# Latent attention opened in a new order: weight splits, value projections and rope of the first heads

## Chip, cores and metric

One of the cores of a Trainium2 chip runs the whole program. Times are microseconds (us) on the device. TensorE is called PE, VectorE DVE, ScalarE ACT, GpSimd POOL and SyncE SP, as in the profile.

## What is computed

A decoder of three blocks in fp32 for 512 rows of width 1024. The change is in the first mixer, multi-head latent attention with 16 heads, with a 512-wide latent for queries and a 256-wide one for keys and values:

```python
h = x @ w_in                                  # 1024 -> 512 + 256 + 32
c_q, c_kv, k_rope = h[..., :512], h[..., 512:768], h[..., 768:]
q = (rms_norm(c_q, q_norm) @ w_uq).reshape(b, s, 16, 64 + 32)
q = jnp.concatenate([q[..., :64], apply_rope(q[..., 64:], pos)], axis=-1)
kv = (rms_norm(c_kv, kv_norm) @ w_ukv).reshape(b, s, 16, 64 + 64)
k_nope, v = kv[..., :64], kv[..., 64:]
k = jnp.concatenate([k_nope, broadcast(apply_rope(k_rope, pos))], axis=-1)
out = dense_causal_attention(q, k, v, 96 ** -0.5) @ w_o
```

Behind it come a layer norm, cross attention over 256 memory rows and a gated FFN; then a block with sparse top-k attention, and a last one with forgetting attention, pooling and a convolutional FFN.

## The kernel before, in words

Every fp32 product is made of three matmuls (`mm3`, lines 153 to 155) on a high and a low half of each operand. `split` makes the two halves of an activation: a cast on ACT (line 160) and a subtraction on DVE (line 161).

Weights are a list of units (`plan`), each of up to 128x1024. `use()` hands out the next unit; before that it sees that `ahead` more units are prepared and that `dma_ahead` more are under way on SP's queue. Preparing one is a cast on ACT to `wh` (line 121) and a subtraction to `wl` (line 122) on `lo_eng`, which is DVE, and POOL during the attention. The units are in order: eight of w_in, two of the rope part of w_uq (`uu`), the values of heads 0 to 7 (`v`), the keys (`k`), the first block of the queries' plain part (`q`, heads 0 to 3), the values of heads 8 to 15 (in the kernel before they replace `v` when `vproj(1, ...)` first asks for them), and the second query block (heads 4 to 7), which `proj(2)` takes.

`mla` (line 482) loads x as four tiles of 128 rows, `setup` loads the constants, `front` transposes tiles (tp, by matmul with the identity) and multiplies them by w_in into pa and pb, and `norm` makes the RMS-normed rows cn: the squares on ACT, a row of short steps for the reciprocal root on DVE, then cn itself (lines 542 to 545). `back` transposes cn and splits it into cq and ckv. `norm(3)` and `back(3)` are those of the last tile. Then rq (the rope part of all queries, two groups of 256 rows), v (values of heads 0 to 7, four blocks of rows, 24 matmuls) and the rope of the keys and of the first queries (`rope`, line 380: a shuffle, two products, a sum and a split).

`proj(p)` makes the keys and queries of head pair p (qk: 6 + 12 matmuls). In `attention` head h goes through scores s (12 matmuls, line 689), a softmax (reductions on DVE, line 692, exponentials on ACT, line 694, the reciprocal on DVE, line 700, products with it on POOL, line 703, in the tiles P and p), transposes t (line 711) two heads later, and the output o three heads later. Behind the scores of head h, `ahead(h)` calls `proj(h//2+1)` for even h; `fill(h)` then runs the values of heads 8 to 15 as `FILL_V` says.

A scheduler orders the instructions of each engine at build time; on the chip each engine runs its own list in that order.

Of the kernel before, what the change touches and what calls it, by code (L numbers as in the profile page):

```python
# [34 lines left out]
FILL_B = {2: 1, 3: 1, 4: 1, 6: 1, 9: 1, 11: 1, 12: 1, 14: 1, 17: 1, 19: 1, 20: 1, 22: 1, 24: 1, 27: 1, 28: 1}  # L35
FILL_V = {1: (0,), 3: (1,), 4: (2, 3)}
FILL_P = {7: (0,), 8: (1,), 9: (2,), 10: (3,)}
# [27 lines left out]
class K:  # L65
# [314 lines left out]
    def rope(self, src, out, eng):  # L380

        nc = self.nc
        t = self.pg(F, "rp")
        t1, t2 = t[:, 0:512], t[:, 512:1024]
        nc.vector.stream_shuffle(t2, src, [(i + 16) % 32 for i in range(32)])
        eng.tensor_tensor(t1, src, self.cos, op=OP.mult)
        eng.tensor_tensor(t2, t2, self.sin, op=OP.mult)
        nc.vector.tensor_tensor(t1, t1, t2, op=OP.add)
        self.split(out[:, 0], out[:, 1], t1)

# [91 lines left out]
    def mla(self):  # L482
# [3 lines left out]
        for t in range(NT):  # L486
            x = self.pg(F, "x0")
            if t == 0:
                nc.scalar.dma_start(x[:, 512:1024], xd[:, t, 512:1024])
                nc.sync.dma_start(x[:, 0:512], xd[:, t, 0:512])  # L490
            else:
                last = nc.sync.dma_start(x, xd[:, t, :])
            xs.append(x)
            self.load(1 if t == 0 else 8)
            if t == 1:
                self.setup(last)
        us = []
# [19 lines left out]
        def front(ts, then=None):  # L517
            xT = [x0T.pop(t) if t in x0T else tr(t) for t in ts]
            pp = [(self.ps("pa"), self.ps("pb")) for _ in ts]
            for k in range(8):  # L520
                if len(us) == k:
                    us.append(self.use(3))
                u = us[k]
                for x, (pa, pb) in zip(xT, pp):
                    l = [x[0][:, k], x[1][:, k]]
                    self.mm3(pa, l, [u[0][:, 0:512], u[1][:, 0:512]], k == 0, k == 7)
                    self.mm3(pb[:, 0:288], l, [u[0][:, 512:800], u[1][:, 512:800]], k == 0, k == 7)
                if k == 4 and then is not None:
                    x0T[then] = tr(then)
            return pp  # L530
# [38 lines left out]
        self.trig()  # L569
        pp += front((3,))  # L570
        back(2, scr[2])
        prev = norm(3, *pp[3])
        self.ahead, self.dma_ahead = 2, 2
        QF = [[self.pair("qf") for _ in range(2)] for _ in range(2)]
# [4 lines left out]
        ropeq, rps = [], []  # L579
        uu = [self.use(), self.use()]  # L580
        for m in range(4):
            rps.append(self.ps("rq"))
        for g in range(2):
            if g == 1:
                back(3, prev)
            for m in range(4):
                for k in range(4):
                    cc = (m % 2) * 128
                    self.mm3(rps[m][:, g * 256:(g + 1) * 256],
                             [uu[m // 2][0][:, k, cc:cc + 128], uu[m // 2][1][:, k, cc:cc + 128]],  # L590
                             [x[:, g * 256:(g + 1) * 256] for x in cqs[k]], k == 0, k == 3)
            if g == 0:
                st = {n: self.use() for n in ("v", "k", "q")}
        V = {}

        def vproj(h, js=range(NT)):
            if h == 1 and js[0] == 0:
                st["v"] = self.use()
            u = st["v"]
            for j in js:  # L600
                p = self.ps("v")
                c = slice(j * 128, j * 128 + 128)
                for k in range(2):
                    self.mm3(p, [x[:, c] for x in ckvs[k]], [u[0][:, k], u[1][:, k]], k == 0, k == 1)
                V[h, j] = self.pair("v")
                self.split(V[h, j][:, 0], V[h, j][:, 1], p)

        kr = self.pair("kr")
        self.rope(krf, kr, nc.vector)
        rsb = [self.pg(F, "rsb") for _ in range(2)]  # L610
        rsb = [rsb[m // 2][:, (m % 2) * 512:(m % 2) * 512 + 512] for m in range(4)]

        def ropes(m):
            rq = self.pair("rq")
            self.rope(rsb[m], rq, nc.vector if m == 0 else nc.gpsimd)
            ropeq.append(rq)
        nc.scalar.copy(rsb[0], rps[0])
        ropes(0)
        for m in range(1, 4):
            nc.scalar.copy(rsb[m], rps[m])  # L620
        for i in range(2):
            nc.scalar.dma_start(KF[i][0][64:96].bitcast(F), kr[64:96].bitcast(F))
            nc.scalar.dma_start(KF[i][1][32:64].bitcast(F), kr[32:64].bitcast(F))
        OT = []
        vproj(0)

# [26 lines left out]
        def ahead(h):  # L653
            if h in (0, 4, 8):
                ropes(h // 4 + 1)
            if h % 2 == 0 and h < 14:
                proj(h // 2 + 1)
        proj(0)
        self.lo_eng = nc.gpsimd

# [1042 lines left out]
```

## Time and profile before

| | us |
|---|---|
| median of 3 runs | 2175.67 |
| lowest and highest | 2175.51, 2180.46 |
| profiled execution | 2170.42 |
| its span | 2168.6 |
| PE busy in it | 2125.2 (98%) |
| DVE, ACT, POOL busy | 1324.1, 925.7, 287.9 |

The profiled execution is one run, 5 us below the median. Times in the rows are from the start of its span. The granted clock of PE was 0.995 of full speed as a mean over the span.

### The profile page before, as it was taken

Reading aid. Unit: us, or ns where it says so; the run is one execution under the profiler, and the core shown is the slowest. Engines: PE = TensorE matmul, PEld = TensorE weight load, DVE = VectorE, ACT = ScalarE, POOL = GpSimd, SP = SyncE. Lnnn points to the kernel's source line nnn. Section 1 sums busy time; section 2 is a strip of 40 time slices with the busy share of each in tenths; the row PEclk is TensorE's granted clock in tenths of the full one; section 3 lists DMA queues with packets and bytes.
Section 4 is the critical chain, followed back from the end, with each engine's and each line's share of the span. In section 5 each row is a group of like instructions: output and inputs, shape, how many; then the busy total and the mean of one; then the engine's idle time right before and its main releaser. Section 6 shows DMA issues by size and latency. Waiting matters only on the chain.

```text
span 2168.6 us, 30013 instructions
## 1 busy us (share of the span) xinstructions
PE 2125.2 (98%) x11492; PEld 1776.7 (82%) x11492; DVE 1324.1 (61%) x2747; ACT 925.7 (43%) x1684; POOL 287.9 (13%) x288
## 2 busy tenths in 40 slices
PE   8999999999999999899999999999999999999998
PEld 7789898988888887775688888888888879888886
DVE  6776566735237267877676845446377677755734
ACT  3687444313225143578734332224224655343521
POOL 0255100000000002476300000000004310000002
PEclk9999999999999999999999999999999999999999
DMA  6123613355324132240332345444320335432311
GB/s 209 49 67 99 205 59 117 96 167 155 97 94 151 54 107 65 77 123 27 125 119 79 117 155 184 136 127 159 104 59 21 88 112 156 146 94 91 126 59 39
DMA packets 254178, 233.82 MB, mean 108 GB/s; under 512 B 14516, under 2 KB 219700, under 8 KB 254036
## 3 DMA queue, kind: packets, MB, share of 16 engines
q1 hardware_dynamic: 246384, 214.19, 32.1%
q10 hardware_dynamic: 7652, 17.73, 2.6%
q8 instruction: 90, 1.47, 0.3%
q14 instruction: 52, 0.43, 0.1%
HBM read 220.81 MB, written 6.82 MB: 105 GB/s over the span
## 4 chain that ended last, share of the span: by engine, by line
PE 53%; DVE 4%; ACT 2%; issue 1%; POOL 0%; DMA 0%; DVEq 0%; ACTq 0%; POOLq 0%
PE fm L154 9%; PE fm L155 9%; PE fm L153 9%; PE acc L153 6%; PE acc L154 6%; PE acc L155 6%; PE s L1252 1%; PE o L153 1%; PE o L154 1%; PE o L155 1%; DVE sc L1172 1%; PE t L1275 1%; PE v L153 1%; DVE qb L1222 1%; DVE m L1169 1%
## 5 line engine op out<-in xcount | busy, mean ns | idle before, releaser
L154 PE MATMUL fm<-xT,wh 128*128 128x512 f32 (+3 forms) x1640 | 588.8, 361 | 0.4
L155 PE MATMUL fm<-xT,wl 128*128 128x512 f32 (+3 forms) x1640 | 588.3, 359 | 0.0
L153 PE MATMUL fm<-xT,wh 128*128 128x512 f32 (+3 forms) x1640 | 587.7, 360 | 0.5 <-ACT wh L121 0.4
L122 DVE TENSOR_TENSOR wl<-raw,wh 128x1024 fp32r<-128x1024 f32 (+1 forms) x299 | 358.3, 1223 | 94.5 <-ACT wh L121 64.4
L121 ACT CAST wh<-raw 128x1024 fp32r<-128x1024 f32 (+2 forms) x339 | 338.9, 1038 | 71.8 <-PE acc L154 18.8
L154 PEld LDWEIGHTS fm<-xT,wh 128*128 128x128 f32 (+2 forms) x1640 | 307.2, 187 | 48.4 <-DVE xT L250 1.6
L155 PEld LDWEIGHTS fm<-xT,wl 128*128 128x128 f32 (+2 forms) x1640 | 307.4, 187 | 47.2 <-DVE wl L122 0.3
L153 PEld LDWEIGHTS fm<-xT,wh 128*128 128x128 f32 (+2 forms) x1640 | 306.4, 187 | 48.2 <-ACT wh L121 0.9
L122 POOL TENSOR_TENSOR wl<-raw,wh 128x1024 fp32r<-128x1024 f32 (+1 forms) x40 | 93.4, 2344 | 1211.3 <-ACT wh L121 610.6
L153 PE MATMUL acc<-wh,hs 128*128 128x512 f32 x528 | 205.6, 389 | 0.0
L154 PE MATMUL acc<-wl,hs 128*128 128x512 f32 x528 | 205.4, 389 | 0.0
L155 PE MATMUL acc<-wh,hs 128*128 128x512 f32 x528 | 204.9, 389 | 0.0
L974 DVE TENSOR_TENSOR hT<-sil,fm 128x512 f32<-128x512 f32 x44 | 30.3, 688 | 228.5 <-PE fm L155 225.7
L973 ACT ACTIVATE sil<-fm 128x512 f32<-128x512 f32 x44 | 26.3, 598 | 300.6 <-PE fm L155 283.5
L153 PEld LDWEIGHTS acc<-wh,hs 128*128 128x128 f32 x528 | 99.1, 188 | 20.5
L957 DVE SCALAR_TENSOR_TENSOR cv<-fm,cw,cv 128x511 f32<-128x511 f32 x88 | 65.8, 748 | 82.2 <-ACT cv L955 81.0
L154 PEld LDWEIGHTS acc<-wl,hs 128*128 128x128 f32 x528 | 99.1, 188 | 20.5
L155 PEld LDWEIGHTS acc<-wh,hs 128*128 128x128 f32 x528 | 99.1, 188 | 20.5
L153 PE MATMUL acc<-wh,ot 128*128 128x512 f32 x288 | 112.5, 391 | 0.0
L155 PE MATMUL acc<-wh,ot 128*128 128x512 f32 x288 | 112.1, 389 | 0.0
L154 PE MATMUL acc<-wl,ot 128*128 128x512 f32 x288 | 112.1, 389 | 0.0
L217 ACT ACTIVATE x<-x,mv 128x1024 f32<-128x1024 f32 x20 | 24.9, 1243 | 147.9 <-DVE mv L216 147.8
(363 smaller groups left out, 3518.7 us busy)
## 6 DMA issues: line engine op xcount, KB each, us to landing
raw<-in_ffn_w_in_dram SPq DMA_DIRECT2D x88, 512.0 KB
mw<-in_mod_w_dram SPq DMA_DIRECT2D x48, 512.0 KB
raw<-in_ffn_w_down_dram SPq DMA_DIRECT2D x44, 512.0 KB
raw<-in_ffn_up_dram SPq DMA_DIRECT2D x44, 512.0 KB
raw<-in_xa_w_kv_dram SPq DMA_DIRECT2D x32, 512.0 KB
raw<-in_ffn_down_dram SPq DMA_DIRECT2D x22, 512.0 KB
raw<-in_xa_w_q_dram SPq DMA_DIRECT2D x16, 512.0 KB
raw<-in_xa_w_o_dram SPq DMA_DIRECT2D x16, 512.0 KB
```

What stands on the lines that cost most here:

```text
L121: self.nc.scalar.copy(hi[:, :n], raw[:, :n])
L122: self.lo_eng.tensor_tensor(lo[:, :n], raw[:, :n], hi[:, :n].bitcast(F), op=OP.subtract)
L153: mm(out, l[0], r[0], start=first, stop=False, **kw)
L154: mm(out, l[0], r[1], start=False, stop=False, **kw)
L155: mm(out, l[1], r[0], start=False, stop=last, **kw)
L217: ops.append(lambda: nc.scalar.activation(x, x, AF.Identity, bias=mv[:, 3:4], scale=mv[:, 2:3]))
L957: nc.vector.scalar_tensor_tensor(y[:, sh:], p[:, :S - sh], w[:, 2 - sh, c:c + 1], y[:, sh:], op0=OP.mult, op1=OP.add)
L973: nc.scalar.activation(s, g, AF.Silu)
L974: nc.vector.tensor_tensor(hT[j // 2][:, j % 2], s, u, op=OP.mult)
L1169: m = v.max(m8, sc[b])
L1172: v.match_replace(sc[b], m8, sc[b], -3.0e38)
L1222: ops.append(lambda o=o, i=i: v.tensor_copy(o, i))
```

## The change

It rewrites the opening of `mla` and moves one transfer in `mod_start`:

- `setup` comes behind all four x loads; the first weight unit is prepared right behind the first tile's transposes, and the first four (k, tile) steps of `front` are taken in another order.
- Behind `front(3)` only what is used is prepared (`ahead` 0): the rope units and `v`; behind `norm(3)` the units k, q and v1 (heads 8 to 15, now a tile of its own); then `ahead` is 2 again, which takes effect at the next `use()`, that of `proj(2)`.
- Value blocks 0 and 1 of heads 0 to 7 come before `back(3)`, blocks 2 and 3 behind the rope. Blocks 0 and 1 of heads 8 to 15 come between `proj(0)` and the attention; the fills keep blocks 2 and 3.
- The rope of the keys and that of the first queries are interleaved; the rows of the keys' rope are copied in two parts.
- The transfer of c (`cc`) is ordered behind ACT's last instruction before the third block.

```diff
-FILL_V = {1: (0,), 3: (1,), 4: (2, 3)}
+FILL_V = {3: (2,), 4: (3,)}
...
             self.load(1 if t == 0 else 8)
-            if t == 1:
-                self.setup(last)
+        self.setup(last)
...
+            for t in ts:
+                xT.append(x0T.pop(t) if t in x0T else tr(t))
+                if not us:
+                    us.append(self.use(0))
...
+            order = [(k, i) for k in range(8) for i in range(len(ts))]
+            if len(ts) == 2:
+                order[:4] = [(0, 0), (1, 0), (0, 1), (1, 1)]
...
         pp += front((3,))
+        self.ahead, self.dma_ahead = 0, 2
+        uu = [self.use(), self.use()]
+        st = {"v": self.use()}
         back(2, scr[2])
         prev = norm(3, *pp[3])
-        self.ahead, self.dma_ahead = 2, 2
+        for n in ("k", "q", "v1"):
+            st[n] = self.use()
+        self.ahead = 2
...
         for g in range(2):
             if g == 1:
+                vproj(0, (0, 1))
                 back(3, prev)
...
-            if g == 0:
-                st = {n: self.use() for n in ("v", "k", "q")}
...
-        self.rope(krf, kr, nc.vector)
...
-        ropes(0)
+        ropeq.append(self.pair("rq"))
+        ks, qs = self.rope_steps(krf, kr, nc.vector), self.rope_steps(rsb[0], ropeq[0], nc.vector)
+        for x, n in ((ks, 1), (qs, 1), (ks, 2), (qs, 1), (ks, 1), (qs, 2)):
+            for _ in range(n):
+                x.pop(0)()
+        krows(0)
...
-        vproj(0)
+        vproj(0, (2, 3))
...
         proj(0)
+        krows(1)
+        vproj(1, (0, 1))
         self.lo_eng = nc.gpsimd
...
-        nc.scalar.dma_start(cc, a["c_2"].rearrange("o (k p) -> p (o k)", p=128))
+        self.after(nc.scalar.dma_start(cc, a["c_2"].rearrange("o (k p) -> p (o k)", p=128)), self.last_act)
```

What the scheduler makes of it, at three places. First DVE at norm(3), whose short steps are lines 182 to 184 and whose result is cn; wl_590, wl_594 and wl_600 are the low halves of the units k, q and v1 (of before: wl_602, wl_658 and wl_664):

```order
L183 TENSOR_TENSOR rs_572<-rs_572 128x2
L184 SCALAR_TENSOR_TENSOR ss_568<-rs_572,ss_568 128x2
L542 SCALAR_TENSOR_TENSOR cn_567<-pa_501,ss_568,nrows_95 128x512
L543 SCALAR_TENSOR_TENSOR cn_567<-pb_502,ss_568,nrows_95 128x256
L545 COPY cn_567<-pb_502 128x128
L122 TENSOR_TENSOR wl_602<-raw_271,wh_601 128x1024
L161 TENSOR_TENSOR cq_111<-tp_675,cq_110 128x2x128
L122 TENSOR_TENSOR wl_658<-raw_289,wh_657 128x1024
L122 TENSOR_TENSOR wl_664<-raw_307,wh_663 128x1024
L161 TENSOR_TENSOR cq_113<-tp_675,cq_112 128x2x128
L161 TENSOR_TENSOR ckv_115<-tp_680,ckv_114 128x2x128
L122 TENSOR_TENSOR wl_670<-raw_661,wh_669 128x1024
```

The same place after the change, from an earlier short step on:

```order
L183 TENSOR_TENSOR rs_572<-rs_572 128x2
L122 TENSOR_TENSOR wl_590<-raw_271,wh_589 128x1024
L184 SCALAR_TENSOR_TENSOR ss_568<-rs_572,ss_568 128x2
L122 TENSOR_TENSOR wl_594<-raw_289,wh_593 128x1024
L182 TENSOR_TENSOR rs_572<-ss_568 128x2
L122 TENSOR_TENSOR wl_600<-raw_307,wh_599 128x1024
L183 TENSOR_TENSOR rs_572<-rs_572 128x2
```

The three subtractions moved from behind cn to between the steps that lead to it, and a fourth (wl_670, the second query block) is gone from here.

Second PE between the last query matmuls of `proj(0)` (qk_818 before, qk_810 after) and the scores of head 0 (s_837 and its neighbours before, s_851 after). Before:

```order
L154 MATMUL qk_818<-cq_113,wh_657 128x512
L155 MATMUL qk_818<-cq_112,wl_658 128x512
L689 MATMUL s_837<-kf_593,qf_589 128x512 x3
L689 MATMUL s_835<-kf_593,qf_589 128x384 x3
L689 MATMUL s_835<-kf_593,qf_589 128x128 x3
```

And after, where the second of two blocks of six value matmuls (the tile v_839; v_829 stands ahead of it) ends at the scores:

```order
L153 MATMUL v_839<-wh_599,ckv_114 128x512
L154 MATMUL v_839<-wl_600,ckv_114 128x512
L155 MATMUL v_839<-wh_599,ckv_115 128x512
L153 MATMUL v_839<-wh_599,ckv_114 128x512
L154 MATMUL v_839<-wl_600,ckv_114 128x512
L155 MATMUL v_839<-wh_599,ckv_115 128x512
L708 MATMUL s_851<-kf_609,qf_605 128x512
L708 MATMUL s_849<-kf_609,qf_605 128x384
```

Twelve value matmuls now stand between the first keys and queries and the first scores.

Third POOL during the first heads; P_974 and p_975 are the softmax of head 2 (P_976 before), and wl_998 is the low half of the second query block, which the matmuls of qk_1028 in `proj(2)` read; wl_931 and wl_1000 of before are units of later use. Before:

```order
L122 TENSOR_TENSOR wl_931<-raw_667,wh_930 128x1024
L703 TENSOR_TENSOR P_907<-P_907,st_909 128x512
L703 TENSOR_TENSOR P_907<-P_907,st_909 128x384
L703 TENSOR_TENSOR P_907<-P_907,st_909 128x128
L703 TENSOR_TENSOR p_908<-p_908,st_909 128x256
L122 TENSOR_TENSOR wl_1000<-raw_673,wh_999 128x1024
L703 TENSOR_TENSOR P_976<-P_976,st_978 128x512
```

And after:

```order
L722 TENSOR_TENSOR P_974<-P_974,st_976 128x512
L722 TENSOR_TENSOR P_974<-P_974,st_976 128x384
L722 TENSOR_TENSOR P_974<-P_974,st_976 128x128
L122 TENSOR_TENSOR wl_998<-raw_597,wh_997 128x1024
L722 TENSOR_TENSOR p_975<-p_975,st_976 128x256
L122 TENSOR_TENSOR wl_1004<-raw_603,wh_1003 128x1024
L122 TENSOR_TENSOR wl_1010<-raw_1001,wh_1009 128x1024
```

Its high half stands on ACT behind the exponentials of the same head:

```order
L713 ACTIVATE P_974,st_976<-P_974,st_976 128x512
L713 ACTIVATE P_974,st_976<-P_974,st_976 128x384
L713 ACTIVATE P_974,st_976<-P_974,st_976 128x128
L121 CAST wh_997<-raw_597 128x1024
```

The preparation of the second query block moved from DVE and ACT ahead of the attention to POOL and ACT within it.

## Rows read from the trace of the kernel before

**Rows 1.** The page, part 1: engine, busy us, share of the span, instructions.
```profile
PE 2125.2 (98%) x11492; PEld 1776.7 (82%) x11492; DVE 1324.1 (61%) x2747; ACT 925.7 (43%) x1684; POOL 287.9 (13%) x288
```

**Rows 2.** Waits of PE, 0 to 200 us: us in total, times, longest.
```profile
PE tp L553 <- DVE cn L542: 3.0, 1, 3.0
...
PE s L689 <- ACT qf L160: 1.7, 1, 1.7
PE pa L153 <- ACT wh L121: 1.4, 1, 1.4
PE tp L509 <- DMA x<-in_x_dram: 1.2, 3, 0.5
...
PE s L689 <- DVE kf L161: 0.2, 1, 0.2
```

**Rows 3.** Stretches: length, busy (count) of PE, PEld, DVE, ACT, POOL; PEclk, DMA, GB/s.
```profile
62.00:67.00 5.00, 5.00 (x25) 4.40 (x24) 4.23 (x6) 3.32 (x7) 0.00 (x0) 0.66 0.00 0
...
83.00:87.00 4.00, 4.00 (x15) 3.42 (x15) 3.45 (x12) 3.45 (x10) 0.41 (x1) 0.57 0.00 0
...
106.00:200.00 94.00, 91.14 (x590) 78.98 (x589) 69.22 (x189) 71.37 (x178) 50.60 (x55) 1.00 0.26 75
200.00:860.00 660.00, 659.76 (x3382) 557.64 (x3381) 358.80 (x666) 233.27 (x348) 34.32 (x24) 1.00 0.37 114
860.00:2150.00 1290.00, 1270.74 (x6965) 1050.92 (x6964) 811.23 (x1679) 560.58 (x1033) 177.28 (x182) 1.00 0.34 106
```

**Rows 4.** Timeline of PE: start, duration, instruction, count, idle before and releaser.
```profile
10.83 0.79 PE L153 MATMUL pa<-wh,x0T 128*128 128x512 f32 x1 [1.43 <-ACT wh L121]
...
14.96 0.40 PE L153 MATMUL pa<-wh,x0T 128*128 128x512 f32 x1
...
61.21 0.63 PE L553 MATMUL tp<-cst,cn 128*128 128x128 f32 x4 [2.96 <-DVE cn L542]
...
74.93 0.39 PE L153 MATMUL qk<-ckv,wh 128*128 128x512 f32 x1
...
89.42 2.06 PE L689 MATMUL s<-kf,qf 128*128 128x512 f32 x12
91.32 0.39 PE L153 MATMUL v<-wh,ckv 128*128 128x512 f32 x1
...
92.70 0.27 PE L711 MATMUL t<-cst,P 128*128 128x128 f32 x1
...
93.71 2.16 PE L689 MATMUL s<-kf,qf 96*128 96x512 f32 x12
95.71 0.40 PE L153 MATMUL qk<-ckv,wh 128*128 128x512 f32 x1
...
99.81 0.40 PE L153 MATMUL o<-pt,v 128*64 128x512 f32 x1
```

**Rows 5.** Timeline of DVE.
```profile
61.57 1.22 DVE L122 TENSOR_TENSOR wl<-raw,wh 128x1024 fp32r<-128x1024 f32 x1
...
85.79 0.73 DVE L385 STREAM_SHUFFLE rp<-rsb 128x512 f32<-128x512 f32 x1
...
88.53 0.68 DVE L161 TENSOR_TENSOR kf<-qk,kf 64x512 fp32r<-64x512 f32 x1
...
97.78 0.68 DVE L692 CUSTOM_DVE_ANT_0 P<-s,cst 128x512 f32<-128x512 f32 x1
...
99.42 0.08 DVE L692 DVE_READ_ACCUMULATOR2_ANT st<- 128x1 f32 x1
```

**Rows 6.** Timeline of POOL.
```profile
89.43 2.61 POOL L703 TENSOR_TENSOR P<-P,st 128x512 f32<-128x512 f32 x3 [1.54 <-ACT rq L160]
92.00 0.61 POOL L703 TENSOR_TENSOR p<-p,st 128x256 f32<-128x256 f32 x1
...
98.07 2.41 POOL L122 TENSOR_TENSOR wl<-raw,wh 128x1024 fp32r<-128x1024 f32 x1
101.15 2.18 POOL L703 TENSOR_TENSOR P<-P,st 128x512 f32<-128x512 f32 x3 [0.67 <-DVE st L700]
```

More of the change, by code (lines that the diff above doesn't have):

```diff
@@ L380, in rope, with rope_steps @@
     def rope(self, src, out, eng):
+        for f in self.rope_steps(src, out, eng):
+            f()
+    def rope_steps(self, src, out, eng):
         nc = self.nc
@@ L384, in rope, with products @@
         t1, t2 = t[:, 0:512], t[:, 512:1024]
[L385 to L389, printed above, removed]
+        def products():
+            eng.tensor_tensor(t1, src, self.cos, op=OP.mult)
+            eng.tensor_tensor(t2, t2, self.sin, op=OP.mult)
+        return [lambda: nc.vector.stream_shuffle(t2, src, [(i + 16) % 32 for i in range(32)]), products,
+                lambda: nc.vector.tensor_tensor(t1, t1, t2, op=OP.add), lambda: self.split(out[:, 0], out[:, 1], t1)]
     def plan(self):
@@ L517, in front @@
         def front(ts, then=None):
-            xT = [x0T.pop(t) if t in x0T else tr(t) for t in ts]
+            xT = []
+            for t in ts:
+                xT.append(x0T.pop(t) if t in x0T else tr(t))
+                if not us:
+                    us.append(self.use(0))
             pp = [(self.ps("pa"), self.ps("pb")) for _ in ts]
-            for k in range(8):
+            order = [(k, i) for k in range(8) for i in range(len(ts))]
+            if len(ts) == 2:
+                order[:4] = [(0, 0), (1, 0), (0, 1), (1, 1)]
+            for k, i in order:
                 if len(us) == k:
                     us.append(self.use(3))
[L523 to L528, printed above, removed]
+                u, x, (pa, pb) = us[k], xT[i], pp[i]
+                l = [x[0][:, k], x[1][:, k]]
+                self.mm3(pa, l, [u[0][:, 0:512], u[1][:, 0:512]], k == 0, k == 7)
+                self.mm3(pb[:, 0:288], l, [u[0][:, 512:800], u[1][:, 512:800]], k == 0, k == 7)
+                if k == 4 and i == len(ts) - 1 and then is not None:
                     x0T[then] = tr(then)
@@ L579, in mla, with vproj @@
         ropeq, rps = [], []
-        uu = [self.use(), self.use()]
         for m in range(4):
             rps.append(self.ps("rq"))
+        V = {}
+        def vproj(h, js=range(NT)):
+            u = st["v1" if h else "v"]
+            for j in js:
+                p = self.ps("v")
+                c = slice(j * 128, j * 128 + 128)
+                for k in range(2):
+                    self.mm3(p, [x[:, c] for x in ckvs[k]], [u[0][:, k], u[1][:, k]], k == 0, k == 1)
+                V[h, j] = self.pair("v")
+                self.split(V[h, j][:, 0], V[h, j][:, 1], p)
         for g in range(2):
             if g == 1:
+                vproj(0, (0, 1))
                 back(3, prev)
@@ L591, in mla @@
                              [x[:, g * 256:(g + 1) * 256] for x in cqs[k]], k == 0, k == 3)
-            if g == 0:
-                st = {n: self.use() for n in ("v", "k", "q")}
[L594 to L606, printed above, removed]
         kr = self.pair("kr")
-        self.rope(krf, kr, nc.vector)
         rsb = [self.pg(F, "rsb") for _ in range(2)]
@@ L616, in ropes, with krows @@
             ropeq.append(rq)
+        def krows(i):
+            nc.scalar.dma_start(KF[i][0][64:96].bitcast(F), kr[64:96].bitcast(F))
+            nc.scalar.dma_start(KF[i][1][32:64].bitcast(F), kr[32:64].bitcast(F))
         nc.scalar.copy(rsb[0], rps[0])
-        ropes(0)
+        ropeq.append(self.pair("rq"))
[4 more added lines that the diff above has]
+        krows(0)
         for m in range(1, 4):
             nc.scalar.copy(rsb[m], rps[m])
-        for i in range(2):
-            nc.scalar.dma_start(KF[i][0][64:96].bitcast(F), kr[64:96].bitcast(F))
-            nc.scalar.dma_start(KF[i][1][32:64].bitcast(F), kr[32:64].bitcast(F))
         OT = []
-        vproj(0)
+        vproj(0, (2, 3))
         def proj(p):
```

## The prediction, made before the changed kernel had run

> **What bounds the kernel now.** I read the page's busy shares first: TensorE (PE) works 2125.2 us of the 2168.6 us span [rows 1], so whatever moves the time either takes idle time from PE or gives it some. The busy time by stretches says where idle time is left. From 200 to 860 us PE stands still for 0.24 of 660 us, and from 860 to the end for 19.3 of 1290 [rows 3], so a lead or a delay that PE has at 200 us is carried to the end nearly whole. The change touches the first 110 us and, apart from one small transfer, nothing later. There the waits of PE are few [rows 2]: 1.4 us for the first weight unit's rounding on ACT, 0.5 (the longest of three) for a tile of x, 3.0 for the third norm's result cn (the norm of rows 384 to 511, called norm(3) in the code), 1.7 and 0.2 for the first head's query and key halves, and from 106 to 200 us another 2.9 us in pieces [rows 3]. Last I read the granted clock: two stretches ran below full speed, 62 to 67 us at a mean of 0.66 and 83 to 87 us at 0.57 [rows 3], each right behind one of the two longest waits; and at the start a 128x512 matmul is still listed at about twice the later 0.40 us until 14.96 us [rows 4]. All that the opening can win is therefore about 1.4 + 0.5 + 3.0 + 1.9 us of waits and 5.0 x 0.34 = 1.7 and 4.0 x 0.43 = 1.7 us of slow clock.
>
> A unit for what follows: 18 projection matmuls of 128x512 take 95.71 to 99.81 us [rows 4], 0.228 us each. A head's twelve score matmuls take 89.42 to 91.32, 1.90 us [rows 4].
>
> **Step 1, the start.** The first weight unit is now rounded between the two x tiles' casts and not behind all four, so PE need not wait 1.43 us at 9.39; and the x tiles no longer queue behind the eight setup transfers on SP's queue, which ends the 0.53 us wait. Gain 1.96. From below: if full clock comes at 14.96 whatever PE did before, the 1.43 are worth half, 1.2 in all. From above: if it comes as much sooner as to spare half of 10.83 to 14.96, 3.0. I take 1.96, since the transposes, which PE began with, stand where they stood. The k-order that goes with it only serves these waits.
>
> **Step 2, norm(3) and the third gap.** Twelve value matmuls, 12 x 0.228 = 2.74 us, move into the 2.96 us that PE waited for cn. But three splits of weights (the low halves for the key, query and second value units) now stand between norm(3)'s short steps on DVE, where they stood behind cn; the order shows it. One takes 1.22 us [rows 5]; 3 x 1.22 = 3.7, of which I take 3.4, as the short steps wait for each other's results and a split fills some of that. The transposes of cn start at 61.21 + 3.4 = 64.6, PE still stands still for 3.6 us, and proj(0), the first head pair's projection, starts at 74.93 + 3.4 - 2.74 = 75.6 instead of 74.93. Loss 0.7, with bounds 0.0 and 1.0. The slow stretch behind this gap stays as it was.
>
> **Step 3, the fourth gap.** Between proj(0) and the first scores stand twelve matmuls of the second value half now. Their 2.74 us cover the 1.9 us in which the query halves were waited for; without that wait I expect no slow stretch there. PE runs 18 projections, 12 values, 12 scores of head 0, 18 projections, 12 scores of head 1: 4.10 + 2.74 + 1.90 + 4.10 + 1.90 = 14.7, ending at 90.4, which was 91.32. With step 1 the lead is 2.9 us, and 2.74 us of value work is done that was to come later: 5.7 in all.
>
> **Step 4, head 0's softmax.** In the kernel before, six value matmuls stood between head 1's scores and head 0's transposes t (91.32 to 92.70), and these came to 93.71 [rows 4]. Now nothing stands there, and the softmax is late: head 0's scores end at 84.3; four reductions on DVE (97.78 to 99.50 in head 2's case, 1.72 [rows 5]), two value splits that now stand among them (some 0.65 each, as the split at 88.53 [rows 5]), then the rope's shuffle, which POOL and through it the reciprocal wait for. From the shuffle to POOL's first product it was 85.79 to 89.43 [rows 5, 6]; 0.6 of these 3.6 were another split (88.53), which has moved. So POOL starts at 90.3, takes 2.57 + 0.61 [rows 6], and t ends at 93.8: 2.5 us of new waiting. Head 2's scores start at 93.8, on the new clock 91.8, where it was 93.71. The lead is now 1.9, and 6 matmuls more are done, 1.4: 3.2.
>
> **Step 5, the stall that I expect.** Heads 4 and 5 need the second block of query weights. Before, it was rounded behind norm(3) (wh_669 on ACT, wl_670 on DVE). Now it is asked for only when proj(2) comes, inside the attention. ACT does its high half after head 2's exponentials, and POOL its low half after three products of head 2's softmax: P_974, P_974, P_974, wl_998 in the order. PE has twelve matmuls of qk_1028 to do right there, the third of which needs wl_998, and behind them on PE stand all of head 0's output, head 1's transposes and head 3's scores. The length comes from the same chain before: head 2's scores end at 95.71 and POOL's third product at 101.15 + 2.18 = 103.3, 7.6 us; one split on POOL is 2.41 [rows 4, 6]: 10.0 us after the scores. In that time PE can do six key matmuls and two query matmuls, 1.8. **Idle: 8.2 us**, from 6.1 (if the 2.07 us between the scores' end and the first reduction at 97.78 are not lost again) to 8.8 (with a p product, 0.61, ahead). Lead 3.2 - 8.2: 5.0 late.
>
> **Step 6, the clock behind the new waits.** Here the rows say 1.7 us for a wait of 3.0 and again for one of 1.9 [rows 2, 3], and 10.83 to 14.96 at half speed, 2.06, at the start [rows 4]. I take 2.2 behind the stall (from 1.7 to 3.4) and 0.8 behind step 4's wait, part of whose slow stretch falls into the stall: 3.0. The Trainium skill, "TensorE: Matmul & The Clock Gate", section "What's actually happening", calls the lower clock the default that activity releases; by that a PE that stood still for long resumes as at launch, which makes 2.1 behind the stall where the two later rows make 1.7. The sum would be 7.9 by the one and 7.5 by the other.
>
> **What costs nothing.** The interleaved rope products are the same instructions on DVE, and the twelve value matmuls give them time. The transfer of c now waits on ACT's queue near 412 us, where PE is covered by 660 us without a gap [rows 3]. Later fills have six matmuls where they had twelve; that is work done early and counted above.
>
> **Sum.** 5.0 + 3.0 = 8.0 us late. Against the profiled execution (2170.42) that is 2178.4; the shown median, 2175.67, lies 5 us higher, and I predict from it: **2183.5 us**. A difference within 0.3%, 6.5 us, is about what a measurement of this kernel cannot tell from none.
>
> **The rivals.** *A, the same stall, partly repaid (0.23):* while PE stands still, ACT and DVE catch up, and the 2.9 us of waits from 106 to 200 us vanish; step 4's clock costs nothing. 8.0 - 2.9 - 0.8 = 4.3: 2180. For it: those waits are for ACT and DVE. Against it: their chains start from PE's results, so they shift with it. *B, the other side, no stall (0.10):* PE's waits are decided at one point, whether wl_998 is ready when the six key matmuls end, 1.4 us after head 2's scores. If it is, the 8.2 and the 2.2 fall away: 2.4 faster, 2173.3, within 0.3%. For it, only that the weights have long landed; against it, the order on POOL and ACT, and a chain of 10.0 us that would have to be 1.4. *C, faster (0.12):* as B, and head 0's softmax in time too, so that 2.5 and 0.8 go as well: 5.7 faster, and with the upper bound of step 1 6.7: 2169. Against it besides: the shuffle behind the two value splits. *D, slower yet (0.10):* each of the three waits brings a slow stretch of its own at the upper bound, 1.7 more behind norm(3) and 1.2 more behind the stall: 10.9, 2186.6. That step 1 does nothing (the tile and the weights come no sooner) would make 2185.5 and lies within the forecast's own range.
>
> **How the numbers follow.** The forecast has 0.45, with its own range 2182.2 to 2187; with D it makes slower 0.55. A and B make same 0.33, C faster 0.12. The range leaves out most of C and little else: 2172 to 2188, B and D and the bounds of steps 1, 2, 5 and 6 within it.
>
> **What the changed profile would show.** Step 1: no idle time ahead of the first pa matmul. Step 2: the wait for cn after the twelve v matmuls, 3.6 us, and three wl rows between norm(3)'s steps. Step 3: no wait ahead of the first s. Step 4: t waiting on POOL's P for about 2.5 us. Step 5: qk waiting some 8 us in total for ACT's wh and then POOL's wl near 95 to 104 us, and head 0's output starting about 6 us later than 99.81. Step 6: a low granted clock behind it. I am wrong if qk's wait is under 4 us, or if the waits between 106 and 200 us shrink by as much as the stall grows.

## The result, and the profile after

The changed kernel takes 2187.12 us (median of 7 runs, 2183.83 to 2196.05), where the kernel before, on the same chip, took 2175.51 (median of 7). The ratio is 1.0059, 95% interval 1.0040 to 1.0077: by the ratio about 12.8 us slower, where 8 were forecast (the two medians differ by 11.6). Slower was right; 2183.5 us was too low: on the median that the forecast started from, 2175.67, the ratio makes 2188.5, just outside its 2172 to 2188. The profiled execution took 2185.65 us with a span of 2183.9.

The page, part 1, of the kernel after (engine, busy us, share of the span, instructions):

```profile
PE 2131.4 (98%) x11492; PEld 1781.8 (82%) x11492; DVE 1326.4 (61%) x2746; ACT 925.2 (42%) x1684; POOL 291.9 (13%) x289
```

The number of matmuls is that of [rows 1]; PE is busy 6.2 us longer with the same matmuls, which points to a lower clock; the rest of the 15.3 us between the spans is idle time. The same matmul, counted from the end of the program, starts 11.64 us later than before at 247.65 us (259.29) and still 11.64 later at 799.61 (811.25). So the opening costs 11.64 us in this execution, and nothing between 250 and 860 us, the transfer of c near 412 us among it, adds or repays any. From 860 to 1016 us another 3.2 are lost against before's profiled execution ("What stays open"). I account for the 11.64.

The waits of PE in the kernel after, 0 to 200 us (total, times, longest):

```profile
PE tp L563 <- DVE cn L552: 5.0, 1, 5.0
...
PE qk L153 <- ACT wh L121: 3.6, 1, 3.6
PE qk L155 <- POOL wl L122: 2.7, 1, 2.7
...
PE t L730 <- POOL P L722: 1.8, 3, 1.0
PE o L154 <- DVE pt L161: 1.3, 1, 1.3
PE pa L154 <- DVE wl L122: 0.5, 1, 0.5
```

Against [rows 2], the first weight's 1.4 us and the scores' 1.7 are gone, the wait for cn has grown from 3.0 to 5.0, and new are 1.8 us for t, 0.5 for pa's second weight half and the two waits of qk, 6.3 us together. Now the stretches of the kernel after (length, busy (count) of PE, PEld, DVE, ACT, POOL; PEclk, DMA, GB/s):

```profile
62.00:68.20 6.20, 5.36 (x22) 4.85 (x23) 4.36 (x11) 1.31 (x4) 0.00 (x0) 0.52 0.01 3
...
90.00:94.00 4.00, 2.61 (x11) 1.89 (x12) 3.95 (x10) 2.50 (x6) 2.58 (x4) 0.73 0.26 71
94.00:98.60 4.60, 4.60 (x16) 4.12 (x16) 1.85 (x6) 3.58 (x11) 0.19 (x1) 0.50 0.01 4
...
103.00:112.50 9.50, 6.62 (x15) 4.44 (x16) 1.49 (x3) 3.67 (x6) 9.27 (x7) 0.51 0.06 14
...
120.00:200.00 80.00, 76.85 (x496) 66.75 (x495) 59.13 (x153) 60.51 (x147) 48.75 (x50) 1.00 0.26 69
```

Three stretches run near half speed, the lower of the two levels (1.2 of 2.4 GHz), one behind each of the three groups of waits. In [rows 3] there were two. The timeline of PE after, at the places of [rows 4] (start, duration, what, idle before and releaser):

```profile
8.98 0.78 PE L153 MATMUL pa<-wh,x0T 128*128 128x512 f32 x1
...
62.84 1.12 PE L563 MATMUL tp<-cst,cn 128*128 128x128 f32 x4 [4.98 <-DVE cn L552]
...
74.61 0.39 PE L153 MATMUL qk<-ckv,wh 128*128 128x512 f32 x1
...
81.41 2.08 PE L708 MATMUL s<-kf,qf 96*128 96x512 f32 x12
...
87.43 2.06 PE L708 MATMUL s<-kf,qf 128*128 128x512 f32 x12
90.48 0.33 PE L730 MATMUL t<-cst,P 128*128 128x128 f32 x1 [0.99 <-POOL P L722]
...
93.83 3.87 PE L708 MATMUL s<-kf,qf 96*128 96x512 f32 x12
97.50 0.63 PE L153 MATMUL qk<-ckv,wh 128*128 128x512 f32 x1
...
103.19 0.80 PE L153 MATMUL qk<-cq,wh 128*128 128x512 f32 x1 [3.59 <-ACT wh L121]
...
107.10 0.80 PE L155 MATMUL qk<-cq,wl 128*128 128x512 f32 x1 [2.69 <-POOL wl L122]
...
111.53 0.63 PE L153 MATMUL o<-pt,v 128*64 128x512 f32 x1
```

The first pa starts at once; the first scores start without a wait; head 2's scores take 3.67 us (93.83 to 97.50) where they took 2.00 before (93.71 to 95.71 [rows 4]); and head 0's output starts at 111.53 instead of 99.81. Behind the last wait, twelve matmuls take from 107.10 to 112.37, 5.27 us, where at 0.228 they would take 2.74. What the second of the two stalled matmuls waited for, the low half, stands on POOL:

```profile
102.56 2.18 POOL L722 TENSOR_TENSOR P<-P,st 128x512 f32<-128x512 f32 x3 [1.40 <-DVE st L719]
104.70 2.35 POOL L122 TENSOR_TENSOR wl<-raw,wh 128x1024 fp32r<-128x1024 f32 x1
```

and what the first waited for, the high half, on ACT behind head 2's last exponential:

```profile
101.73 0.39 ACT L713 ACTIVATE P<-P,st 128x128 f32<-128x128 f32 x1
...
102.11 1.97 ACT L121 CAST wh<-raw 128x1024 fp32r<-128x1024 f32 x2
```

Neither preparation depends on the softmax; each merely comes behind it in its engine's list. (The low half also needs the high one, which is there at 103.2 us.)

### The profile page after: what moved, and what is told of

Same layout as the page of the kernel before. It is cut to its first block, busy times and chain, and to the rows that moved or that the text cites. A ratio compares the mean times of both kernels' runs of the same rounds, so it can differ in the third digit from the quotient of the medians.

```text
span 2183.9 us, 30018 instructions
## 1 busy us (share of the span) xinstructions
PE 2131.4 (98%) x11492; PEld 1781.8 (82%) x11492; DVE 1326.4 (61%) x2746; ACT 925.2 (42%) x1684; POOL 291.9 (13%) x289
## 3 DMA queue, kind: packets, MB, share of 16 engines
q1 hardware_dynamic: 246384, 214.19, 32.2%
## 4 chain that ended last, share of the span: by engine, by line
PE 53%; DVE 4%; ACT 2%; DMA 1%; issue 0%; POOL 0%; SPq 0%; ACTq 0%; DVEq 0%; POOLq 0%
PE fm L154 9%; PE fm L155 9%; PE fm L153 9%; PE acc L153 6%; PE acc L155 6%; PE acc L154 6%; PE s L1271 1%; PE o L153 1%; PE o L154 1%; PE o L155 1%; DVE sc L1191 1%; DVE qb L1241 1%; PE v L153 1%; PE t L1294 1%; DVE m L1188 1%; PE v L155 1%
## 5 line engine op out<-in xcount | busy, mean ns | idle before, releaser
L121 ACT CAST wh<-raw 128x1024 fp32r<-128x1024 f32 (+2 forms) x339 | 338.5, 1038 | 68.2 <-PE acc L154 19.1
```

What stands on the lines that cost most here:

```text
L121: self.nc.scalar.copy(hi[:, :n], raw[:, :n])
```

## The experiments

"Shift" is how much later (or earlier) than in the kernel before the same matmul starts near 800 us; in the kernel after it is +11.64. A trace reads to some hundredths there, but it is one execution, and two executions of the same instructions were up to 3.0 us apart through the clock (below); the timed ratio resolves about 0.1 to 0.2%, 2 to 4 us. Where the ratios of two kernels overlap, I go by the trace and the clock in it.

### Is it the late query block?

**The second query block prepared behind back(3), the rest as changed.**

```diff
                 back(3, prev)
+                self.ensure(self.cur + 1)
```

> The changed kernel with one line more: the second query block (heads 4 to 7) is prepared behind back(3), on ACT and DVE, as early as in the kernel before. Theory 1 (late weights): PE's two waits in qk at 99.6 and 104.4 us (3.59 and 2.69) vanish and with them most of the slow clock from 103 to 112.4 (2.5 us lost) and 0.8 of slow matmuls between the waits; head 0's output starts near 102 to 103 instead of 111.53, so the attention is 8 to 9.5 us sooner than in the changed kernel and only 2 to 3.5 us later than before: time about 2178. Rival 2 (the norm): what counts is the 4.98 us wait for cn and the slow clock behind it and behind the transposes; the waits in qk are replaced by waits for the softmax of the same heads, and 2 us or less is won.

2180.22 us (9 runs), ratio 1.0023 (1.0008 to 1.0038), shift +1.7. Both qk waits are gone and 10 of the 11.64 us with them. Its timeline of PE:

```profile
89.66 0.33 PE L731 MATMUL t<-cst,P 128*128 128x128 f32 x1 [1.06 <-POOL P L723]
...
92.45 2.15 PE L709 MATMUL s<-kf,qf 96*128 96x512 f32 x12
94.44 0.40 PE L153 MATMUL qk<-ckv,wh 128*128 128x512 f32 x1
```

and its stretches behind cn and at head 0's transposes:

```profile
62.00:68.20 6.20, 5.51 (x30) 4.92 (x31) 5.34 (x11) 2.13 (x5) 0.00 (x0) 0.72 0.01 3
...
90.00:94.00 4.00, 2.95 (x18) 2.33 (x19) 3.95 (x9) 2.40 (x6) 1.76 (x3) 1.00 0.09 18
```

The wait ahead of t is as long as in the kernel after (1.06, 0.45, 0.37 and 0.24 us here, 0.99, 0.45 and 0.37 there), but here the clock stayed at 1.00. From the first t to the end of head 2's scores this kernel takes 4.78 us, the kernel after 7.02: the slow clock costs 2.2 us there. Behind cn too, after the same wait of 5.0 us, the clock from 62 to 68.2 us is 0.72 here and 0.52 there (6.2 x 0.20 = 1.2 us). So the 10 us are 6.3 of waits and 2.5 of clock behind them, 2.2 and 1.2 of a clock that fell less behind equal waits, less 2.4 of new waits (1.4 for p ahead of later transposes, 1.0 for ot ahead of scores). The 3.4 us of clock are not this edit's doing, as the next run shows. Without them the edit is worth about 6.4 us by these numbers; the timed ratio fell by 0.0036, 7.8 us, and the two intervals lie apart, if only just.

**The same one head later**, asked for behind head 1's scores:

```diff
         def ahead(h):
+            if h == 1:
+                self.ensure(self.cur + 1)
```

> The changed kernel with the second query block asked for one head sooner, behind head 1's scores, still on ACT and POOL. Its low half then stands among the products of head 1 (P_921) and not behind those of head 2. If the stall is head 2's softmax and one split in a row, it ends about 7 us sooner: POOL's split at about 99 to 102 us, PE's wait in qk 0 to 2.5 us in place of 6.3, and the attention is 5 to 9 us sooner than in the changed kernel. Rival: POOL's 2.4 us and ACT's 1.05 in the middle of head 1's softmax make its transposes late by as much, and less than 4 us are won.

Shift +4.54; 2184.5 us (4 runs), ratio 1.0048 (1.0034 to 1.0062), which alone does not tell it from the kernel after. The wait for ACT's half is gone, that for POOL's stays at 2.83 us, above the 0 to 2.5 expected. One head sooner frees one of the two halves, as each is decided by its own engine's list.

This run also settles a question of the clock. PE has the same instructions in the same order here as in the kernel after until past head 2's scores, the other engines until those have begun, and PE's waits are the same (4.97 us for cn; 1.00, 0.45, 0.37 and a new 0.24 at t). Its clock is not:

```profile
62.00:68.00 6.00, 5.20 (x27) 4.65 (x28) 4.31 (x10) 1.38 (x4) 0.00 (x0) 0.72 0.01 3
...
90.00:99.00 9.00, 5.67 (x30) 4.01 (x29) 7.31 (x18) 7.44 (x19) 5.36 (x6) 1.00 0.06 14
```

In the same two stretches the kernel after has 0.50 and 0.62. Head 2's scores end at 94.46 us, in the kernel after at 97.50. So 3.0 of the 11.64 us come from a clock that the same list, with the same waits, did not bring a second time. Of the 7.1 us by which this trace is ahead, only 4.1 are left for the edit.

**The kernel before, with its second query block asked for late.** Only `proj(2)` asks for it, as in the changed kernel.

```diff
-                st = {n: self.use() for n in ("v", "k", "q")}
+                st = {n: self.use(1) for n in ("v", "k", "q")}
...
-                st["v"] = self.use()
+                st["v"] = self.use(0)
```

> The kernel before with one thing of the change alone: the second query block is asked for only by proj(2). Here the scheduler puts its high half on ACT ahead of head 2's exponentials and its low half on POOL ahead of P, and three output matmuls into the gap. If the lateness of the demand is what costs, PE waits as in the changed kernel, 6 us and a slow clock, 8 to 10 us later than before. If the place behind head 2's softmax is what costs, the low half is ready some 4.6 us after head 2's scores end at 95.7 (transposes split, one cast of 1.05, one split of 2.4 us), PE waits 2 to 3.5 us for it, and the kernel is 2 to 5 us later than before.

2176.14 us (10 runs), ratio 1.0007 (0.9996 to 1.0018), shift -0.2. Its waits of PE, 0 to 200 us:

```profile
PE t L711 <- POOL p L703: 1.3, 1, 1.3
PE qk L155 <- POOL wl L122: 1.2, 1, 1.2
...
PE s L689 <- ACT qf L160: 0.7, 1, 0.7
```

This falsifies the short form of my reason, "asked for late, hence a stall", and is milder than either expectation (2 to 3.5 us of waiting were the lower one). Here the scheduler put the low half ahead of head 2's products on POOL:

```profile
95.46 0.61 POOL L703 TENSOR_TENSOR p<-p,st 128x256 f32<-128x256 f32 x1
96.03 2.38 POOL L122 TENSOR_TENSOR wl<-raw,wh 128x1024 fp32r<-128x1024 f32 x1
99.11 2.18 POOL L703 TENSOR_TENSOR P<-P,st 128x512 f32<-128x512 f32 x3 [0.70 <-DVE st L700]
```

In the kernel after it stands behind the same three products. So lateness alone does not cost the 6 us; the place in the lists does, as far as this pair shows, which differs in other things too. And an ACT and DVE that no longer prepare the block ahead of the first heads even cut the wait for the query half from [rows 2]'s 1.7 us to 0.7.

### Is it the fills?

**Six value matmuls back as a fill behind head 1's scores.**

```diff
-FILL_V = {3: (2,), 4: (3,)}
+FILL_V = {1: (1,), 3: (2,), 4: (3,)}
...
-        vproj(1, (0, 1))
+        vproj(1, (0,))
```

> The changed kernel with six of the twelve value matmuls of heads 8 to 15 put back behind head 1's scores, as a fill, and six left between proj(0) and the scores. If the wait of 1.8 us for POOL's products and the slow clock from 90 to 98.6 us behind it (2.8 us lost, the term that the prediction had at 0.8) come from nothing standing there, both go: head 2's scores take 2.0 and not 3.67 us, and the attention is 3.5 to 4.6 us sooner than in the changed kernel. Rival: the slow clock has its cause in the gap before (57.9 to 62.8) or comes at the first scores, and 1.8 us or less is won.

2187.8 us (4 runs), ratio 1.0061 (1.0041 to 1.0082), shift +11.31. The t wait falls to 1.0 us, head 2's scores run at full clock and end 2.7 us sooner, and the qk waits grow from 6.3 to 7.5 (4.8 and 2.7). The low half is ready only 1.3 us sooner, since head 2's softmax still queues behind head 1's on DVE and ACT. What PE wins ahead of the stall, the stall mostly takes back: 0.3 us arrive, where 3.5 to 4.6 were expected.

### Is it the splits behind the last norm?

**The three splits ordered behind cn.** A dependence on cn's last instruction is added to each.

```diff
+        self.hold = self.last_split
         for n in ("k", "q", "v1"):
             st[n] = self.use()
+        self.hold = None
...
+        if self.hold is not None:
+            self.after(ins, self.hold)
```

> The changed kernel with the three low halves of k, q and v1 ordered behind cn on DVE, as the heads of the change's words have it. Rival 2: the wait for cn goes from 4.98 to about 1.6 us (4.98 less three splits at 1.13 start to start), the slow clock behind it, 2.6 us lost, shrinks or goes, and all behind it is 3.4 to 6 us sooner than in the changed kernel. Theory 1: the same gain at proj(0), carried on, since the stall in qk starts from PE's own scores; the two waits in qk stay at 6.3 us and the kernel stays slower than before by 5.5 to 8 us. If nothing arrives at head 3, the stall is set by something else than PE's scores.

The waits of PE:

```profile
PE rq L157 <- DVE cq L164: 2.3, 1, 2.3
PE tp L566 <- DVE cn L555: 1.9, 1, 1.9
```

The wait for cn falls from 5.0 to 1.9, as the three splits between norm(3)'s steps made it long. But a new one of 2.3 comes behind it: the halves of cq now queue behind the splits on DVE, and the two waits in qk are 7.1 us. Shift +9.33, so 2.3 us better than the kernel after, less than the 3.4 to 6 expected; the ratio, 1.0066 (1.0044 to 1.0088, 4 runs), shows no gain.

**The rotary table behind norm(3).**

```diff
-        self.trig()
         pp += front((3,))
...
         prev = norm(3, *pp[3])
+        self.trig()
```

> The changed kernel with the steps of the rotary table put behind norm(3) in the code; the order then has norm(3) right behind the third norm on DVE, the table behind it, and the three weight splits behind the table. If the table and the splits together make the wait for cn (the kernel with the start alone shows the table's part), cn is ready when the twelve value matmuls end, the 4.98 us go, with them the slow clock from 62.8 to 68.2 (2.6 us lost), and the kernel is 5 to 7.6 us sooner than the changed one at the attention, still 4 to 6.6 us later than before, since the stall in qk stays. Rival: the table and the splits then come late for the rope, PE waits at head 0's scores for it, and less than 3 us are won.

Shift +8.56, 3.1 us better than the kernel after where 5 to 7.6 were expected; ratio 1.0063 (1.0042 to 1.0084, 4 runs), again no gain in the time. The wait for cn is gone altogether, and rq waits 2.4 us for ACT's cast of cq and 0.7 for DVE's half. This edit moves the table and the splits; as the splits alone left 1.9 us, the rest was the table's. Timeline of DVE after:

```profile
43.15 0.92 DVE L175 TENSOR_SCALAR rs<-rs 128x2 int32<-128x2 int32 x1
...
46.78 0.75 DVE L552 SCALAR_TENSOR_TENSOR cn<-pa,ss,nrows 128x512 f32<-128x512 f32 x1
...
56.05 0.43 DVE L377 TENSOR_SCALAR trig<-trig 128x512 f32<-128x512 f32 x1
56.43 0.16 DVE L547 TENSOR_TENSOR ss<-ss,cst 128x2 f32<-128x2 f32 x1
...
62.04 0.75 DVE L552 SCALAR_TENSOR_TENSOR cn<-pa,ss,nrows 128x512 f32<-128x512 f32 x1
```

norm(3) starts the moment the table's last product ends. PE was 3.1 us earlier than before by then, norm(3) only 1.3 (57.74 before). Why the table came late stands in the first two lines and on POOL:

```profile
43.09 0.94 POOL L593 MEMSET kf<- 32x1024 f32 x1
```

The norm before it, norm(2), takes 4.41 us from its first step (42.37) to cn (46.78), in the kernel before 2.57. Four of its steps take 0.55 to 0.92 us instead of 0.17 while POOL clears the buffers of the keys and queries (42.13 to 45.87), which before was done by 44.16, ahead of norm(2) at 45.53. Every run with the memsets at that place has the 4.4 us; the start alone and the two runs with the splits on POOL, where they stand elsewhere, have 2.57; in the first of those two norm(3) then starts at 54.54. So this overlap holds up the table, and with it norm(3), by 1.8 us.

**The splits on POOL**, with the second query block there too and the fill as above.

```diff
+        self.lo_eng = nc.gpsimd
         for n in ("k", "q", "v1"):
             st[n] = self.use()
+        self.lo_eng = nc.vector
```

> The changed kernel with the second query block prepared behind back(3), the four low halves of k, q, v1 and that block on POOL (which is idle there) and not on DVE, and six value matmuls back as a fill. With e7, where the waits only moved along DVE's list (61.2 rq, 79.2 s), the theory is that DVE's work before head 0's scores is what is short: four splits of 1.22 us less on it, cn comes about 3.3 us sooner than in the changed kernel, the wait for it is 1.3 to 1.7, and against the kernel before the attention is 3 to 6 us sooner; time about 2170 to 2172, 0.15 to 0.3 per cent faster. Rival: POOL's splits of 2.4 us each come too late for the keys and queries of heads 0 and 1 or hold DVE up, and it is no sooner than the kernel before.

Shift +3.44; 2181.96 us (6 runs), ratio 1.0030 (1.0018 to 1.0042): later than the first experiment's +1.7, where 3 to 6 us sooner than before were expected. The wait for cn grows to 6.5 us though DVE has no split left to do. Its DVE:

```profile
55.54 2.40 DVE L183 TENSOR_TENSOR rs<-rs 128x2 f32<-128x2 f32 x1
57.98 2.26 DVE L184 SCALAR_TENSOR_TENSOR ss<-rs,ss 128x2 f32<-128x2 f32 x1
60.28 2.26 DVE L182 TENSOR_TENSOR rs<-ss 128x2 f32<-128x2 f32 x1
62.57 0.16 DVE L183 TENSOR_TENSOR rs<-rs 128x2 f32<-128x2 f32 x1
```

and its POOL:

```profile
55.52 7.00 POOL L122 TENSOR_TENSOR wl<-raw,wh 128x1024 fp32r<-128x1024 f32 x3 [54.37 <-DVE rs L182]
```

Three steps of two elements a row each last as long as one split on POOL.

**The same with the table behind norm(3).**

> The same with the rotary table behind norm(3) as well. If DVE's list is what is short, this adds nothing or loses up to 2 us against the former run, since the table's steps then stand ahead of the rope (the wait for cn goes, one for the rope's queries at head 0 comes). Rival: the wait for cn is the last that counts there, and another 1.3 to 1.7 us are won.

Shift +6.73, 3.3 us worse than the former where up to 2 were allowed for; 2178.97 us (11 runs), ratio 1.0020 (1.0012 to 1.0029), which does not show that loss. The first scores wait 7.5 us for the query half: DVE's rope products, 0.68 us alone, take 2.88 beside POOL's memsets and 3.21 beside a memset and a split.

**The first edit, the fill and the table together.**

> The changed kernel with three edits: the second query block prepared behind back(3), the table behind norm(3), and six value matmuls back as a fill behind head 1's scores. If the three losses are separate, their gains add: about 10 (measured alone), 5 to 7.6, and 2 from the wait for POOL's products; against the kernel before, 5 to 8 us sooner at the attention, time about 2168 to 2170, faster by 0.25 to 0.4 per cent. Rival: one wait takes the place of another (the rope, head 0's queries, the transposes behind POOL), and it ends within 2 us of the kernel before.

Shift +1.95; 2178.5 us (11 runs), ratio 1.0023 (1.0014 to 1.0033): nothing beyond the first edit alone, as the rival had it. rq waits 2.4 us for cq and the scores 2.0 and 0.3 for qf. From 50 to 90 us DVE is busy for 32.2 of 40 us and ACT for 22.0; neither is full, but the chain to the first scores runs through both, and each removed wait comes back further down.

### What was good in the change?

**The start alone, on the kernel before:** `setup` behind the x loads, the first weight behind the first tile's transposes, the new order of four (k, tile) steps.

```diff
-            if t == 1:
-                self.setup(last)
+        self.setup(last)
...
+                if not us:
+                    us.append(self.use(0))
...
+            order = [(k, i) for k in range(8) for i in range(len(ts))]
+            if len(ts) == 2:
+                order[:4] = [(0, 0), (1, 0), (0, 1), (1, 1)]
```

> The kernel before with only the start of the change: setup behind the x loads, the first weight unit between the tiles' casts, the k-order. PE is 3.1 us ahead at the first query rope matmuls, as in the changed kernel's profile. Theory a (the table holds the norm): norm(3) on DVE waits for the rotary table, whose steps end at 56.45 instead of 57.76, so cn comes only 1.3 us sooner, PE's wait for it grows from 2.96 to about 4.8, and the attention is 1.3 us sooner than before. Rival b: norm(3) follows PE, and 3.1 us arrive. In the time 0.06 or 0.14 per cent, so the profile decides.

2171.92 us (10 runs), ratio 0.9989 (0.9979 to 1.0000), shift -1.05. PE is 2.7 us earlier at the first rq (49.59, before 52.26), but then waits 3.2 for cn and 2.8 for the rope's rows in qf (where 1.7 and 0.2 stood before head 0's scores): 1.05 are left after head 0's scores. That is near theory a's 1.3, but not by its mechanism. The table ends at 55.40, 2.4 us sooner than before and not 1.3, norm(3) starts right there, and the wait for cn is 3.2 and not 4.8. Here nothing draws norm(2) out; what is lost is lost at head 0's scores.

**The start and the late query block, on the kernel before.**

> The kernel before with the start of the change and the second query block asked for by proj(2) only, the two edits that alone cost nothing there (1.05 and 0.2 us sooner at the attention). The fourth split of 1.22 us is then off DVE ahead of the rope, and head 0's scores, which waited 2.78 us for the rope's queries with the start alone, should wait about 1.5. If so, PE is 2.2 to 3 us sooner than in the kernel before from 200 us on, and the time is 2171 to 2173, faster by 0.1 to 0.15 per cent. Rival: the wait for POOL's low half in qk (1.15 us) grows by what is won ahead of it, and 1.1 us or less remain.

2172.61 us (11 runs), ratio 0.9990 (0.9981 to 1.0000), shift -3.08. Its waits of PE:

```profile
PE tp L558 <- DVE cn L547: 3.3, 1, 3.3
...
PE qk L155 <- POOL wl L122: 1.2, 1, 1.2
...
PE s L694 <- ACT qf L160: 0.7, 1, 0.7
```

PE is 2.9 us sooner at the first rq (49.36) and, with the second block out of the way of the first heads, 3.1 sooner at 800. That is not one lead kept whole: without a slow stretch at head 0's scores (clock 0.97 from 60 to 110 us) it grows to 5.7, and the waits for POOL's products and low half take the rest back. By its trace it is the best of these kernels; by the timed ratio, 0.1%, it is at the edge of what can be told from no change.

### What stays open

In several of the runs derived from the kernel after, the timed ratio is larger than the shift at 800 us (one head sooner: 1.0048 is 10.4 us, the shift 4.5). Their traces lose the rest in the top-k stage, where every kernel has the same instructions in the same order. Before, that stage:

```profile
905.00:1000.00 95.00, 89.12 (x877) 69.48 (x877) 74.92 (x249) 72.15 (x207) 64.08 (x65) 0.98 0.32 96
```

and in the first experiment:

```profile
905.00:1000.00 95.00, 87.80 (x782) 70.22 (x784) 67.62 (x218) 62.48 (x179) 56.62 (x59) 0.87 0.31 93
```

The granted clock there differs from execution to execution, 0.87 to 0.98 here, and it shifts what follows by up to 11 us (in the kernel with the splits behind cn). The profiled execution of the kernel before lost least, so a comparison behind 860 us leans against all the others. No order by the time of arrival shows: read over the stretch moved by the shift, the clock is 0.88 in the kernels 1.7 and 4.5 us late and 0.97 in the one 6.7 us late. What decides it, these runs don't tell. Nor did I run the value blocks' new places and the interleaved rope each alone.

## Why the prediction was right about the direction and short in size

The step that failed is step 6, the clock behind the waits: 0.8 us behind step 4's wait, measured 2.2, and step 2's slow stretch that "stayed as it was", 0.8 more. Of the rest, the misses ahead of proj(0) cancel by luck, and the others stay under 1 us. I follow PE's milestones; each predicted time is the one of the step, less step 1's 1.96.

- **Step 1, the start**, was worth 3.1 us at 52.9 us, not 1.96: the upper bound. The reason given for the middle (the transposes stand where they stood) was wrong. With no wait between the transposes and pa, matmuls run at 0.39 from 10.09 us, not from 14.96. But it gave nothing more by 62.84, since norm(3) could not start before the table was through: PE waits 4.98 us instead of 3.6. The prediction let cn follow PE and had no term for the 1.8 us that norm(2) loses beside the memsets. The three splits cost 3.0 us (norm(3) takes 5.61 to cn, 2.57 before), not 3.4. That the transposes of cn start at 62.84, predicted 62.6, is luck: the larger gain, the memsets and the cheaper splits cancel.
- **Step 2, the slow stretch behind cn**, did not "stay as it was". It lasts from 62.84 to 68.2 at 0.52; proj(0) starts at 74.61, predicted 73.6, so it costs 0.8 us more. In the kernel with the block one head sooner, with the same list, the stretch ran at 0.72 and the 0.8 did not come: head 0's scores start at 80.61 there, at 81.41 in the kernel after.
- **Step 3** held: no wait ahead of the first scores; head 1's scores end at 89.49, predicted 88.4, the late 1.1 of the above.
- **Step 4, the wait for POOL's products**, came as argued, 1.8 us where 2.5 were said; t and head 2's scores end at 97.50. From the end of head 1's scores that is 8.0 us; predicted were 5.3 and, in step 6, 0.8 for the clock. Measured against the first experiment, 2.2 of it is the clock.
- **Step 5, the stall**, was right in place, order and length: low half ready 9.6 us after head 2's scores, predicted 10.0. The idle time is 6.3 us and not 8.2, 0.4 by the shorter chain and the rest because the matmuls inside it ran slowly, which costs nothing there.
- **Step 6, "0.8 behind step 4's wait, part of whose slow stretch falls into the stall"**, is the term that was mis-sized. It measured 2.2. The slow matmuls that fall into the stall do cost nothing, but head 2's scores lie ahead of the stall, and the whole chain that ends it (reductions, exponentials, products, split) starts from them. Every tenth by which they run late lengthens the path. But the 2.2 belong to this execution: the same list with the same waits ran there at full clock a second time (one head sooner), so a wait of this size can bring 0 or 2.2, and the prediction took one number for it. Behind the stall the clock cost 2.5 (107.10 to 112.37), predicted 2.2.
- **"That is work done early and counted above"**, said of the later fills: not quite. Where the fill has six matmuls instead of twelve there is now a wait of 1.3 us for pt at 135.30, where 0.58 stood before; 0.9 us with what goes with it. That the smaller fill is its cause is argued from the place; no run has twelve there again.

Together: 0.2 + 0.8 + 0.1 behind the norm, 1.9 in step 4 and its clock, -0.4 in the stall, 0.3 behind it, 0.9 from the fill: 3.8, and 8.0 + 3.8 = 11.8 against 11.64. Of the 3.8 us, 2.5 are clock (0.8, 1.4 in step 4, 0.3) and 0.9 is what the fill no longer covers; the stall itself was 0.4 shorter than forecast. With the clock of the kernel one head sooner the same path would give about 8.6 (11.64 - 3.0), an estimate that no run of the kernel after shows. "Carried to the end nearly whole" held to 860 us, not behind it: 3.2 us more went in the stage with the changing clock. And 2175.67 + 8.0 is 2183.7, not 2183.5.

Of the rivals, A (partly repaid) fell: from 120 to 200 us PE still stands still for 3.15 us, where 2.9 were from 106 on [rows 3]. B and C (no stall) fell with the order of POOL and ACT. D (a slow stretch of its own behind each of three waits) came nearest in mechanism and time, 2186.6; it had the extra clock behind norm(3) and the stall, where most of it stood behind step 4's wait.

The prediction's sentence on the Trainium skill, "TensorE: Matmul & The Clock Gate", section "What's actually happening" (the lower clock is the default, which activity releases), had a resume as at launch behind the stall. The trace agrees as far as it goes: behind each of the stall's two parts the first matmul is listed at 0.80 us, as the first pa was at 0.78.

## What to carry to other kernels

When preparation is asked for later, look at what stands ahead of it in the list of the engine that does it: a late demand cost 1.2 us of waiting in front of a softmax's products and 6 behind them. Price the low clock behind a new wait by what starts from the slowed matmuls: if the next stall's chain begins there, the slow time is on the path in full. Give it a range that includes nothing, and look for a second execution of the same list before you call a clock an effect of the edit. And where the chain to the next consumer runs through two busy engines, as DVE and ACT here, expect a wait that is removed to come back there, and judge an edit by how far PE's lead survives downstream, not by the wait it removed.

## What the runs showed of the hardware that was not expected

- **A tiny DVE step can last as long as a POOL split.** DVE's steps on 128x2 elements took 2.40, 2.26 and 2.26 us instead of 0.16 while POOL ran three splits. The Trainium skill, "SBUF — State Buffer", section "Who interferes with whom", says that a DVE instruction with two SBUF inputs contends with a GpSimd one that reads SBUF, and calls the port pair that they share an exclusive lock. The trace agrees: with splits of 7.00 / 3 = 2.33 us, each step waited about one out. Beside memsets of 0.95 us, too, norm(2)'s TENSOR_SCALAR steps took 0.55 to 0.92 us in the kernel after.
- **An equal wait, two clocks.** About 2 us of waits ahead of head 0's transposes were followed by a half-speed stretch in the kernel after and by none in the kernel one head sooner, with the same instructions on every engine up to there (1.00 and, from 94 to 98.6 us in the kernel after, 0.50). A wait of 5.0 us for cn and a slow stretch behind it, at 0.52 in the one and 0.72 in the other, went before in both. So the program and its waits do not decide it alone; what does, no run here shows.
- **The clock at the start** rose some 5 us sooner (10.09, not 14.96 us) once PE had no wait between its first transposes and its first products.
